# First projection of a two-layer decoder: input taken in halves of channels, with the loads, transposes and first weight reordered

## The chip, the cores and the metric

The kernel runs on one core of one Trainium2 chip. Its time is the device time of one execution in microseconds (us), given as the median of several executions; lower is better. Beside the timed runs there is one profiled execution, whose span goes from its first to its last instruction. Engines are named as in the profile: PE (TensorE, matmuls; PEld its weight loads), ACT (ScalarE), DVE (VectorE), POOL (GpSimd), SP (SyncE, which here only issues transfers).

## The reference

A decoder trunk of two layers works on x of 512 tokens by 1024 channels in float32. Layer 0 is dilated sliding-window attention and a gated feed-forward with a short convolution; layer 1 is a forgetting attention over keys and values made once, and the same feed-forward. Only the very beginning matters here: the norm of the input and the first projection.

```python
def rms_norm(x, g):
    x32 = x.astype(jnp.float32)
    y = x32 * lax.rsqrt(jnp.mean(x32 * x32, axis=-1, keepdims=True) + EPS)
    return (y * g.astype(jnp.float32)).astype(x.dtype)

def dilated_mixer(xn, w_qkv, w_o, cos, sin):
    B, T, _ = xn.shape
    qkv = xn @ w_qkv                      # (512, 1024) @ (1024, 2304)
    q, k, v = jnp.split(qkv, 3, axis=-1)
    q = apply_rope(q.reshape(B, T, A_HEADS, HEAD_DIM), cos, sin)
    ...
# reference(): mix = dilated_mixer(rms_norm(h, g[0]), w_qkv_a[l], w_o_a[l], cos, sin), h = x at first
```

## The kernel before, in words

**Precision.** Every float32 operand of a matmul is split in a high part, rounded to the matmul's format (`fp32r`), and a low part, the rest. A product is three matmuls: high by high, high by low, low by high (`mm3`, L282 to L285).

**The first stage** computes q and k of the first head group for all 512 tokens: 4 blocks of 128 tokens (b) by 512 columns, each the sum over 8 chunks of 128 channels (kc), so 4 x 8 x 3 = 96 matmuls into four PSUM banks (`qk_ps`). Channels must lie on the partitions, so x is transposed on PE in 128 x 128 pieces, 4 x 8 = 32 of them, four to a PSUM bank (`xt_ps`). ACT copies a bank to the high part (`xah`, line L1268), DVE subtracts that from the bank for the low part (`xal`, L1272). The gains are folded into the weight: ACT scales a piece of w by the gain of its channel (`W.high`, L64), DVE makes the low part in one instruction (`W.low`, L82). The rows' own factor (the root mean square, `rstd0`, L1060 to L1062: a square and sum on ACT, a root, a reciprocal on DVE) is applied when the bank is read (`qk_post`, L1094), where POOL then rotates q and k (rope, L1100 to L1103).

**Weights.** The class `Weights` goes through a list of pieces of 128 x 1024 numbers (512 KB). Pieces 0 to 3 are the first stage's weight, two chunks kc each, loaded as two transfers of 256 KB; pieces 4 and 5 are v of the same group; from 6 on come the other groups. `load(n)` issues transfers up to piece n, `high`, `low`, `split` make the parts, `get` hands a pair to PE. The first six raw pieces lie in tiles of their own (`wearly`, two pieces to a tile `early[i]`).

**What sets the order.** There is no scheduler: the program's order is each engine's order (`manual_schedule`), and an engine that waits holds all that stands behind it. All transfers of this stage are issued by SP in program order: the gains of the norm (4 KB, L235), x block 0 (512 KB, L225), pieces 0 and 1, x block 1, piece 2, x block 2, piece 3, the rope table, x block 3, and so on. There are eight semaphores for such transfers; a transfer is issued only when the one eight places ahead of it has landed.

**PE's order at the start.** Three warm-up matmuls on zeros (L243, 128 x 512 bf16), the transpose of the gains (L260), five more warm-ups, the eight transposes of block 0, two warm-ups, then qk of block 0, kc 0, 1 and 2; the eight transposes of block 1; block 0, kc 3; block 1, kc 0 to 3; transposes of block 2; block 0, kc 4 and 5, block 1 the same; transposes of block 3; kc 6 and 7 of blocks 0 and 1; then all 24 matmuls of block 2 and all 24 of block 3. After that comes the v projection (`v_proj0`, tile `v_ps`), with transposes of the rotated q and k in between (`qk_transpose`, L1109, blocks 0 and 1 after half of it, 2 and 3 at its end).

**POOL's order** after its masks: rope of block 0 and of block 1, eight copies that bring blocks 0 and 1 in the order of tokens of the other groups (`reorder`, L1083), rope of blocks 2 and 3, four more such copies.

Of the kernel before, what the change touches and what calls it, by code (L numbers as in the profile page):

```python
# [9 lines left out]
F32 = mybir.dt.float32  # L10
F32R = mybir.dt.float32r
BF16 = mybir.dt.bfloat16
AF = mybir.ActivationFunctionType
ALU = mybir.AluOpType

D = 1024
T = 512
NB = 4
KD = D // 128
# [98 lines left out]
def trunk_kernel(ctx, tc, x, norm_gains, w_qkv_a, w_o_a, w_q_b, w_o_b, kv_norm, w_kvf, b_f,  # L118
                 w_up, conv_w, conv_b, w_down, rope, out):
    nc = tc.nc  # L120
    act, dve, pool, pe, sp = nc.scalar, nc.vector, nc.gpsimd, nc.tensor, nc.sync
# [8 lines left out]
    def t8(shape, dt=F32, name="t8"):  # L130
        return p8.tile(shape, dt, tag="t8", name=name)

    def t4(shape, dt=F32, name="t4"):
        return p4.tile(shape, dt, tag="t4", name=name)
# [4 lines left out]
    def bank(shape, name="bank"):  # L139
        return psp.tile(shape, F32, tag="ps", name=name)  # L140
# [4 lines left out]
    xv, outv = x[0], out[0]  # L145
# [62 lines left out]
    early = []  # L208
# [8 lines left out]
    W = Weights(nc, new_raw, lambda: t8([128, 2, 1024], F32R, name="w"), pieces)  # L217
# [3 lines left out]

    h = cst.tile([128, NB, D], F32, name="h")

    def load_x(b):
        sp.dma_start(h[:, b, :], xv[b * 128:(b + 1) * 128, :])  # L225

    def load_gain(src, name):
        t = t4([128, D], name=name)
# [2 lines left out]

    eps_t = cst.tile([128, 1], F32, name="eps_t")
    dve.memset(eps_t, EPS)
    g_row = sml.tile([8, 128], F32, tag="grow", name="g_row", bufs=1)
    sp.dma_start(g_row, norm_gains[0, 0].rearrange("(k p) -> k p", p=128))  # L235

    zero = t2([128, 512], BF16, name="zero")
    dve.memset(zero, 0.0)
# [2 lines left out]
    def warm_up(n):  # L241
        for i in range(n):
            pe.matmul(warm, zero[:, 0:128], zero, start=True, stop=True)  # L243
    load_x(0)
    W.load(2)
    load_x(1)
    W.load(3)
    load_x(2)
    W.load(4)
    rp = t4([128, 8, 32], name="rope")  # L250
    sp.dma_start(rp, rope)
    load_x(3)
    act.activation(sml.tile([128, 1], F32, tag="sd", name="warm"), eps_t, AF.Sqrt)

    ident = cst.tile([128, 128], F32, name="ident")
    make_identity(nc, ident)

    warm_up(3)
    pg0 = bank([128, 8], name="g_ps")
    pe.transpose(pg0, g_row, ident[:8, :8])  # L260
    gcol0 = sml.tile([128, 8], F32, tag="gcol0", name="gcol0", bufs=1)
    dve.tensor_copy(gcol0, pg0)
    warm_up(5)

    def columns(*ks):
        return [gcol0[:, k:k + 1] for k in ks]
# [4 lines left out]
    for s in range(2):  # L271
# [6 lines left out]
    pool.affine_select(mask0[:, 128:256], mask0[:, 128:256], pattern=[[-1, 128]], compare_op=ALU.is_ge,  # L278
                       fill=NEG, base=0, channel_multiplier=1)
    same = cst.tile([128, 4], F32, name="same")  # L280

    def mm3(o, ah, al, bh, bl, first, last, shared=False):  # L282
        pe.matmul(o, ah, bh, start=first, stop=False, skip_group_check=shared)  # L283
        pe.matmul(o, ah, bl, start=False, stop=False, skip_group_check=shared)  # L284
        pe.matmul(o, al, bh, start=False, stop=last, skip_group_check=shared)  # L285
# [57 lines left out]
    def new_xT(name):  # L343
        hi = [t8([128, 4, T], F32R, name=f"{name}h{i}") for i in range(2)]
        lo = [t8([128, 4, T], F32R, name=f"{name}l{i}") for i in range(2)]
        return hi, lo
# [17 lines left out]
    def xs(xT, kc, s):  # L364
        return xT[0][kc // 4][:, kc % 4, s], xT[1][kc // 4][:, kc % 4, s]
# [686 lines left out]
    xT = new_xT("xa")  # L1052
# [4 lines left out]
    def rstd0(b):  # L1057
        ss, sd = small(1, "s1"), small(1, "sd")
        junk = t2([128, D], BF16, name="junk")
        act.activation(junk, h[:, b, :], AF.Square, scale=1.0 / 32, accum_out=ss)  # L1060
        act.activation(sd, ss, AF.Sqrt, bias=eps_t)
        dve.reciprocal(rt[:, 0, b:b + 1], sd)  # L1062

    def factors_out():
        act.dma_start(rd.rearrange("(b p) -> p b", p=128), rt[:, 0])
# [10 lines left out]
    def reorder(copy, *blocks, parts=(0, 1)):  # L1076

        for i in parts:
            for b in blocks:
                for part in range(2):  # L1080
                    src = by_fourth(xT[part][i][:, :, b * 128:b * 128 + 128])
                    dst = xP[part][i].rearrange("p k (r l) -> p k r l", r=4)[:, :, :, b * 32:b * 32 + 32]
                    copy(dst, src.bitcast(F32))  # L1083

    def ax(g, b, kc):
        return xs(xP if g else xT, kc, slice(b * 128, b * 128 + 128))
# [3 lines left out]
    def qk_post(g, b, o):  # L1090
        if b == 0:
            qks[g] = t8([128, 4, 8, HD], name=f"qk{g}")
        qk = qks[g][:, b]
        act.activation(qk.rearrange("p a d -> p (a d)"), o, AF.Identity, scale=factor(g, b))  # L1094
        tu = t2([128, 2, 8, 16], name="tu")
        rb = 4 * min(g, 1) + b
        c2 = rp[:, rb, None, 0:16].to_broadcast([128, 8, 16])
        s_lo = rp[:, rb, None, 16:24].to_broadcast([128, 8, 8])
        s_hi = rp[:, rb, None, 24:32].to_broadcast([128, 8, 8])
        pool.tensor_tensor(tu[:, 0], qk[:, :, 0:16], c2, ALU.mult)  # L1100
        pool.tensor_tensor(tu[:, 1, :, 0:8], qk[:, :, 8:16], s_lo, ALU.mult)
        pool.tensor_tensor(tu[:, 1, :, 8:16], qk[:, :, 0:8], s_hi, ALU.mult)
        pool.tensor_tensor(qk[:, :, 0:16], tu[:, 0], tu[:, 1], ALU.add)  # L1103
# [151 lines left out]
    W.ahead = 1  # L1255
    ws, qk_banks = {}, {}

    def transposed0(b):
        pts = []
        for i in range(2):  # L1260
            pt = bank([128, 4, 128], name="xt_ps")
            for k in range(4):
                pe.transpose(pt[:, k, :], h[:, b, (4 * i + k) * 128:(4 * i + k + 1) * 128], ident)
            pts.append(pt)
        return pts

    def high0(b, pts, i):
        act.copy(xT[0][i][:, :, b * 128:b * 128 + 128], pts[i])  # L1268

    def low0(b, pts, i):  # L1270
        s = slice(b * 128, b * 128 + 128)
        dve.tensor_tensor(xT[1][i][:, :, s], pts[i], xT[0][i][:, :, s].bitcast(F32), ALU.subtract)  # L1272

    def qk0(b, *kcs):
        if b not in qk_banks:
            qk_banks[b] = bank([128, T], name="qk_ps")
        for kc in kcs:
            s, k = kc // 2, kc % 2
            if s not in ws:
                ws[s] = [t.rearrange("p (k c) -> p k c", k=2) for t in W.get()]  # L1280
            wh, wl = ws[s]
            ah, al = ax(0, b, kc)
            mm3(qk_banks[b], ah, al, wh[:, k, :], wl[:, k, :], kc == 0, kc == KD - 1)

    def split0(b):
        pts = transposed0(b)
        for i in range(2):
            high0(b, pts, i)
            low0(b, pts, i)

    pts = transposed0(0)
    warm_up(2)
    high0(0, pts, 0)
    low0(0, pts, 0)
    W.high()
    W.low()
    high0(0, pts, 1)
    qk0(0, 0, 1)
    W.high()
    W.low()  # L1300
    low0(0, pts, 1)
    qk0(0, 2)
    pts = transposed0(1)
    for i in range(2):
        high0(1, pts, i)
        low0(1, pts, i)
    qk0(0, 3)
    rstd0(0)
    W.split(3)
    qk0(1, 0, 1, 2, 3)  # L1310
    split0(2)
    rstd0(1)
    qk0(0, 4, 5)
    W.split(4)
    qk0(1, 4, 5)
    split0(3)
    qk0(0, 6, 7)
    qk_post(0, 0, qk_banks[0])
    W.split(5)
# [8 lines left out]
    rstd0(2)  # L1328
    rstd0(3)
    reorder(pool.tensor_copy, 0, 1)  # L1330
    qk0(2, *range(8))
    qk_post(0, 2, qk_banks[2])
    factors_out()
    qk0(3, *range(8))
    W.ahead = 4
    qk_post(0, 3, qk_banks[3])
    reorder(pool.tensor_copy, 2, 3, parts=(1,))
# [377 lines left out]
    for n in range(N + 3):  # L1715
        live = n < N
        if live:
            j, i = units[n]
# [96 lines left out]
```

## Time and profile before

| | us |
|---|---|
| median of 3 runs | 1103.9 |
| lowest and highest of them | 1103.11, 1105.02 |
| the profiled execution's own time | 1105.67 |
| its span | 1103.9 |
| PE busy in it | 1094.8 |

A row of the order of time gives the start, how long the first to the last of the row's instructions took, engine, line, operation, the tiles it writes and reads, shapes and count, and in brackets how long the engine had been idle and what ended that. A row of the busy times by stretch gives the stretch, its length, the busy time of PE, PEld, DVE, ACT and POOL with the instructions begun, the clock, the share of the transfer engines and GB/s. A row of groups ends with count, busy time and mean ns of one, and idle time before. A row of the chain is a start, a length and what ran. Matmuls are pipelined: the distance from one start to the next is what one costs in a row of them, not its own duration.

### The profile page before, as it was taken

How to read it: one execution, taken by the hardware profiler on the slowest of the kernel's cores; microseconds unless marked ns; L12 is line 12 of the kernel's file. 1: busy time of each engine (PE TensorE's matmuls, PEld its weight loads, DVE VectorE, ACT ScalarE, POOL GpSimd, SP SyncE). 2: the span in 40 equal slices, each digit the busy share in tenths (PEclk: the TensorE clock that was granted, in tenths of full speed). 3: DMA queues.
4: the chain of work that ended last, by engine and by line, in shares of the span. 5: the costliest groups of instructions: out<-in, count | busy, mean ns of one | idle time of the engine just before them, and what ended most of it. 6: DMA issues, size and time to landing. Idle time of an engine off the chain costs nothing.

```text
span 1103.9 us, 18085 instructions
## 1 busy us (share of the span) xinstructions
PE 1094.8 (99%) x6605; PEld 952.2 (86%) x6605; DVE 873.4 (79%) x1497; ACT 671.0 (61%) x1115; POOL 172.6 (16%) x245
## 2 busy tenths in 40 slices
PE   9999999999999999999999999999999999999997
PEld 6988889899999988888878888889899999988886
DVE  5697788888788779898587666868888788779894
ACT  6654565656666647576552488746656666647572
POOL 2632000311111211000000211100311111211000
PEclk9999999999999999999999999999999999999999
DMA  9699864378887979884446866784368887989872
GB/s 322 175 351 411 321 185 135 79 184 197 205 189 181 248 249 321 319 294 145 134 153 211 274 185 193 241 261 133 82 178 200 201 192 181 235 269 319 315 248 77
DMA packets 191553, 242.66 MB, mean 220 GB/s; under 512 B 12784, under 2 KB 138728, under 8 KB 191464
## 3 DMA queue, kind: packets, MB, share of 16 engines
q1 hardware_dynamic: 175848, 189.33, 53.0%
q0 software_dynamic: 14944, 52.18, 20.7%
q8 instruction: 52, 0.85, 0.3%
q14 instruction: 37, 0.30, 0.1%
q10 hardware_dynamic: 672, 0.00, 0.0%
HBM read 172.37 MB, written 39.73 MB: 192 GB/s over the span
## 4 chain that ended last, share of the span: by engine, by line
PE 94%; DMA 2%; issue 2%; DVE 1%; ACT 1%; SPq 0%; POOL 0%; DVEq 0%; POOLq 0%; ACTq 0%
PE up L285 12%; PE up L283 12%; PE up L284 12%; PE acc L283 9%; PE acc L284 9%; PE acc L285 9%; PE v_ps L283 2%; PE v_ps L285 2%; PE v_ps L284 2%; PE qk_ps L284 2%; PE qk_ps L283 2%; PE qk_ps L285 2%; PE first L285 1%; PE first L283 1%; PE first L284 1%
## 5 line engine op out<-in xcount | busy, mean ns | idle before, releaser
L283 PE MATMUL acc<-w 128*128 128x512 f32 (+1 forms) x311 | 120.6, 388 | 0.3 <-DVE mix L332 0.3
L285 PE MATMUL acc<-w 128*128 128x512 f32 (+1 forms) x311 | 120.4, 387 | 0.0
L284 PE MATMUL acc<-w 128*128 128x512 f32 (+1 forms) x267 | 103.2, 387 | 0.0
L285 PE MATMUL up<-xsh,w 128*128 128x256 f32 x352 | 99.7, 283 | 0.2 <-DMA w<-wsum 0.2
L283 PE MATMUL up<-xsh,w 128*128 128x256 f32 x352 | 99.6, 283 | 0.0
L284 PE MATMUL up<-xsl,w 128*128 128x256 f32 x352 | 99.6, 283 | 0.0
L78 DVE TENSOR_TENSOR w<-wraw,w 128x1024 fp32r<-128x1024 f32 x62 | 82.2, 1349 | 21.2 <-ACT w L60 16.8
L620 ACT ACTIVATE bb<-up,conv 128x512 f32<-128x512 f32 x80 | 59.7, 776 | 59.3 <-DVE up L1007 48.4
L284 PE MATMUL up<-xbl,w 128*128 128x512 f32 (+1 forms) x276 | 93.5, 339 | 0.0
L284 PE MATMUL up<-xcl,w 128*128 128x512 f32 (+1 forms) x276 | 93.5, 339 | 0.0
L283 PE MATMUL up<-xbh,w 128*128 128x512 f32 (+1 forms) x276 | 93.5, 339 | 0.0
L283 PE MATMUL up<-xch,w 128*128 128x512 f32 (+1 forms) x276 | 93.5, 339 | 0.0
L285 PE MATMUL up<-xbh,w 128*128 128x512 f32 (+1 forms) x276 | 93.4, 339 | 0.0
L285 PE MATMUL up<-xch,w 128*128 128x512 f32 (+1 forms) x276 | 93.4, 338 | 0.0
L60 ACT CAST w<-wraw 128x1024 fp32r<-128x1024 f32 x81 | 83.3, 1048 | 16.5 <-PE v_ps L284 6.9
L283 PEld LDWEIGHTS acc<-w 128*128 128x128 f32 x311 | 58.4, 188 | 12.5 <-DVE mix L332 0.7
L285 PEld LDWEIGHTS acc<-w 128*128 128x128 f32 x311 | 58.4, 188 | 11.9
L285 PEld LDWEIGHTS up<-xsh,w 128*128 128x128 f32 x352 | 67.6, 192 | 0.4 <-DMA w<-wsum 0.4
L283 PEld LDWEIGHTS up<-xsh,w 128*128 128x128 f32 x352 | 67.6, 192 | 0.0
L284 PEld LDWEIGHTS up<-xsl,w 128*128 128x128 f32 x352 | 67.6, 192 | 0.0
L621 DVE SCALAR_TENSOR_TENSOR bb<-up,conv,bb 128x511 f32<-128x511 f32 x80 | 59.5, 743 | 6.5 <-ACT bb L620 6.5
L623 DVE SCALAR_TENSOR_TENSOR bb<-up,conv,bb 128x510 f32<-128x510 f32 x80 | 59.9, 748 | 2.8
(310 smaller groups left out, 3110.1 us busy)
## 6 DMA issues: line engine op xcount, KB each, us to landing
wraw<-in_w_up_dram SPq DMA_DIRECT2D x88, 512.0 KB
w<-wraw POOLq DMA_DIRECT2D x32, 512.0 KB, 6.4
dT<-dsums SPq DMA_DIRECT2D x28, 512.0 KB
w<-wsum POOLq DMA_DIRECT2D x24, 512.0 KB, 5.6
dsums<-in_w_down_dram SPq DMA_DIRECT2D x22, 512.0 KB
dsums<-in_w_down_dram SPq DMA_DIRECT2D x44, 256.0 KB
hD<-hc POOLq DMA_DIRECT2D x44, 256.0 KB, 7.0
dact<-hD SPq DMA_DIRECT2D x44, 256.0 KB
```

Source lines behind the costliest of these rows:

```text
L60: (copy or self.nc.scalar.copy)(pair[:, 0], raw)
L78: self.nc.vector.tensor_tensor(pair[:, 1], raw, pair[:, 0].bitcast(F32), ALU.subtract)
L283: pe.matmul(o, ah, bh, start=first, stop=False, skip_group_check=shared)
L284: pe.matmul(o, ah, bl, start=False, stop=False, skip_group_check=shared)
L285: pe.matmul(o, al, bh, start=False, stop=last, skip_group_check=shared)
L620: act.activation(bb[:, s, :], ps, AF.Identity, bias=cp[:, 3, ch:ch + 1], scale=cp[:, 2, ch:ch + 1])
L621: dve.scalar_tensor_tensor(bb[:, s, 1:], ps[:, :T - 1], cp[:, 1, ch:ch + 1], bb[:, s, 1:], ALU.mult, ALU.add)
L623: dve.scalar_tensor_tensor(bb[:, s, 2:], ps[:, :T - 2], cp[:, 0, ch:ch + 1], bb[:, s, 2:], ALU.mult, ALU.add)
```

## The change

Everything computed stays the same: 96 matmuls, 32 transposes, the same parts and scales. What changes is the size of x's transfers and the order.

- **Transfers.** x comes as eight halves (128 tokens by 512 channels, 256 KB). SP issues the first half of block 0 first, then piece 0, then the first halves of blocks 1, 2 and 3. The gains are issued by ACT. POOL copies one number from piece 0's first half into piece 1's place, so piece 1 is not issued before piece 0's first half has landed; it stands ahead of the second halves of blocks 0 and 1, piece 2, the second halves of blocks 2 and 3, the rope table and piece 3.
- **Warm-ups.** Four ahead of the gains' transpose and one behind the first transposes: five instead of ten.
- **Transposes** come by halves: four for block 0, four for block 1, eight for blocks 2 and 3; the second halves are taken for blocks 0 and 1 together, and for 2 and 3 together.
- **First weight.** Chunk 0 of piece 0 is scaled on DVE (`tensor_scalar`), chunk 1 on ACT as before; high and low parts come chunk by chunk between the parts of x.
- **PE's matmuls**: block 0 and 1 on kc 0 and 1 one by one as the parts come (`one0`), then kc 0 and 1 of blocks 2 and 3, kc 2 and 3 of blocks 0 and 1, the second halves' transposes of 0 and 1, kc 2 and 3 of blocks 2 and 3, the second halves' transposes of 2 and 3; kc 4 to 7 of blocks 0 and 1, then of block 2, then of block 3. The statistics of blocks 0 and 1 stand further back on ACT.

```diff
-    def load_x(b):
-        sp.dma_start(h[:, b, :], xv[b * 128:(b + 1) * 128, :])
+    def load_x(i, *blocks):
+        s = slice(i * 512, (i + 1) * 512)
+        for b in blocks:
+            sp.dma_start(h[:, b, s], xv[b * 128:(b + 1) * 128, s])
...
+    load_x(0, 0)
     g_row = sml.tile([8, 128], F32, tag="grow", name="g_row", bufs=1)
-    sp.dma_start(g_row, norm_gains[0, 0].rearrange("(k p) -> k p", p=128))
+    act.dma_start(g_row, norm_gains[0, 0].rearrange("(k p) -> k p", p=128))
...
-    load_x(0)
-    W.load(2)
-    load_x(1)
-    W.load(3)
-    load_x(2)
-    W.load(4)
+    W.load(1)
+    load_x(0, 1, 2, 3)
     rp = t4([128, 8, 32], name="rope")
-    sp.dma_start(rp, rope)
-    load_x(3)
...
-    warm_up(3)
+    warm_up(4)
     pg0 = bank([128, 8], name="g_ps")
     pe.transpose(pg0, g_row, ident[:8, :8])
...
-    warm_up(5)
...
+    pool.tensor_copy(early[0][:, 1, 0:1], early[0][:, 0, 0:1])
+    W.load(2)
+    load_x(1, 0, 1)
+    W.load(3)
+    load_x(1, 2, 3)
+    sp.dma_start(rp, rope)
+    W.load(4)
...
+    def split0(i, *blocks):
+        pts = [transposed0(b, i) for b in blocks]
+        for b, pt in zip(blocks, pts):
+            high0(b, i, pt)
+            low0(b, i, pt)
+
+    def first_weight(k):
+
+        s, g = slice(512 * k, 512 * k + 512), columns(k)[0]
+        if k == 0:
+            dve.tensor_scalar(w0[:, 0, s], raw0[:, s], g, None, ALU.mult)
+        else:
+            act.activation(w0[:, 0, s], raw0[:, s], AF.Identity, scale=g)
+
+    def first_low(k):
+        s, g = slice(512 * k, 512 * k + 512), columns(k)[0]
+        dve.scalar_tensor_tensor(w0[:, 1, s], raw0[:, s], g, w0[:, 0, s].bitcast(F32), ALU.mult, ALU.subtract)
...
+    raw0, w0 = W.raw.pop(0), W.new_pair()
+    W.ready[0] = (w0[:, 0], w0[:, 1])
+    W.n_split = 1
+    pt = transposed0(0, 0)
+    warm_up(1)
+    high0(0, 0, pt)
+    first_weight(0)
+    first_low(0)
+    first_weight(1)
+    one0(0, 0, 0)
+    one0(0, 0, 1)
+    low0(0, 0, pt)
+    one0(0, 1, 0)
+    first_low(1)
+    one0(0, 0, 2)
+    split0(0, 1)
+    one0(0, 1, 1)
+    one0(0, 1, 2)
+    qk0(1, 0)
+    split0(0, 2, 3)
     W.high()
     W.low()
...
+    qk0(1, 1)
+    for b in (2, 3, 0):
+        qk0(b, *((2, 3) if b == 0 else (0, 1)))
+    qk0(1, 2, 3)
+    split0(1, 0, 1)
+    W.split(3)
+    qk0(2, 2, 3)
     rstd0(0)
-    W.split(3)
-    qk0(1, 0, 1, 2, 3)
-    split0(2)
+    qk0(3, 2, 3)
+    split0(1, 2, 3)
+    W.split(4)
     rstd0(1)
     qk0(0, 4, 5)
-    W.split(4)
     qk0(1, 4, 5)
-    split0(3)
     qk0(0, 6, 7)
...
-    qk0(2, *range(8))
+    qk0(2, 4, 5, 6, 7)
     qk_post(0, 2, qk_banks[2])
     factors_out()
-    qk0(3, *range(8))
+    qk0(3, 4, 5, 6, 7)
```

`one0(b, kc, n)` is one of the three matmuls of `mm3` for block b and chunk kc (n = 0 high by high, 1 x high by weight low, 2 x low by weight high), and `qk0` calls it for whole chunks.

More of the change, by code (lines that the diff above doesn't have):

```diff
@@ L1256, in trunk_kernel @@
     ws, qk_banks = {}, {}
[L1258 to L1270, printed above, removed]
-        s = slice(b * 128, b * 128 + 128)
-        dve.tensor_tensor(xT[1][i][:, :, s], pts[i], xT[0][i][:, :, s].bitcast(F32), ALU.subtract)
@@ L1274, in qk0, with transposed0, high0, low0 @@
-    def qk0(b, *kcs):
+    def transposed0(b, i):
+        pt = bank([128, 4, 128], name="xt_ps")
+        for k in range(4):
+            pe.transpose(pt[:, k, :], h[:, b, (4 * i + k) * 128:(4 * i + k + 1) * 128], ident)
+        return pt
+    def high0(b, i, pt):
+        act.copy(xT[0][i][:, :, b * 128:b * 128 + 128], pt)
+    def low0(b, i, pt):
+        s = slice(b * 128, b * 128 + 128)
+        dve.tensor_tensor(xT[1][i][:, :, s], pt, xT[0][i][:, :, s].bitcast(F32), ALU.subtract)
+    def split0(i, *blocks):
[3 more added lines that the diff above has]
+            low0(b, i, pt)
@@ new lines, in first_weight, with weight0 @@
+    def first_weight(k):
[7 more added lines that the diff above has]
+        dve.scalar_tensor_tensor(w0[:, 1, s], raw0[:, s], g, w0[:, 0, s].bitcast(F32), ALU.mult, ALU.subtract)
+    def weight0(s):
+        if s not in ws:
+            ws[s] = [t.rearrange("p (k c) -> p k c", k=2) for t in W.get()]
+        return ws[s]
@@ L1275, in qk0, with one0 @@
+    def one0(b, kc, n):
         if b not in qk_banks:
             qk_banks[b] = bank([128, T], name="qk_ps")
+        w, a = weight0(kc // 2), ax(0, b, kc)
+        pe.matmul(qk_banks[b], a[n == 2], w[n == 1][:, kc % 2, :], start=kc + n == 0, stop=kc + n == KD + 1)
+    def qk0(b, *kcs):
         for kc in kcs:
[L1278 to L1294, printed above, removed]
+            for n in range(3):
+                one0(b, kc, n)
+    raw0, w0 = W.raw.pop(0), W.new_pair()
+    W.ready[0] = (w0[:, 0], w0[:, 1])
+    W.n_split = 1
+    pt = transposed0(0, 0)
@@ L1295, in trunk_kernel @@
+    warm_up(1)
[14 more added lines that the diff above has]
+    split0(0, 2, 3)
     W.high()
     W.low()
[L1297 to L1306, printed above, removed]
@@ L1307, in trunk_kernel @@
-    qk0(0, 3)
+    qk0(1, 1)
[5 more added lines that the diff above has]
+    qk0(2, 2, 3)
     rstd0(0)
-    W.split(3)
-    qk0(1, 0, 1, 2, 3)
-    split0(2)
+    qk0(3, 2, 3)
+    split0(1, 2, 3)
+    W.split(4)
     rstd0(1)
     qk0(0, 4, 5)
-    W.split(4)
     qk0(1, 4, 5)
-    split0(3)
     qk0(0, 6, 7)
```

## The prediction

> **What bounds the kernel now.** I read the page first (share of the engines, then the chain that ended last), then the first 35 us in order of time, the busy times by stretch with the bytes moved, and last POOL's own order.
>
> ```profile
> span 1103.9 us, 18085 instructions
> PE 1094.8 (99%) x6605; PEld 952.2 (86%) x6605; DVE 873.4 (79%) x1497; ACT 671.0 (61%) x1115; POOL 172.6 (16%) x245
> PE 94%; DMA 2%; issue 2%; DVE 1%; ACT 1%; SPq 0%; POOL 0%; DVEq 0%; POOLq 0%; ACTq 0%
> ```
>
> PE is busy 99% and carries 94% of the chain; 9.1 us of the span are left without it. So a change in the first stage is worth what it does to one moment: when PE passes from the last `qk_ps` matmul to `v_ps`. Behind it nearly everything waits for PE and shifts with it.
>
> ```profile
> 0.74 0.40 SPq L235 DMA_DIRECT2D g_row<-in_norm_gains_dram  x1
> 1.20 0.36 SPq L225 DMA_DIRECT2D h<-in_x_dram  x1
> 1.22 1.46 PE L243 MATMUL warm<-zero 128*128 128x512 bf16 x3 [1.22 <-DVE zero L238]
> ...
> 2.61 0.27 PE L260 MATMUL g_ps<-ident,g_row 8*128 8x8 f32 x1
> 2.81 2.31 PE L243 MATMUL warm<-zero 128*128 128x512 bf16 x5
> 4.81 1.62 PEld L1263 LDWEIGHTS xt_ps<-ident,h 128*128 128x128 f32 x8 [0.59 <-DMA h<-in_x_dram]
> 4.92 1.92 PE L1263 MATMUL xt_ps<-ident,h 128*128 128x128 f32 x8
> 6.02 0.59 ACT L1268 CAST xah<-xt_ps 128x512 fp32r<-128x512 f32 x1 [3.79 <-PE xt_ps L1263]
> 6.50 1.34 ACT L64 ACTIVATE w<-wearly,gcol 128x512 fp32r<-128x512 f32 x2
> 6.63 0.82 PE L243 MATMUL warm<-zero 128*128 128x512 bf16 x2
> 6.64 0.69 DVE L1272 TENSOR_TENSOR xal<-xt_ps,xah 128x512 fp32r<-128x512 f32 x1 [3.55 <-ACT xah L1268]
> 7.26 1.42 DVE L82 SCALAR_TENSOR_TENSOR w<-wearly,gcol,w 128x512 fp32r<-128x512 f32 x2
> 7.28 0.50 PE L283 MATMUL qk_ps<-w,xah 128*128 128x512 f32 x1
> ...
> 9.11 0.40 PE L285 MATMUL qk_ps<-w,xal 128*128 128x512 f32 x1
> 9.61 1.46 ACT L64 ACTIVATE w<-wearly,gcol 128x512 fp32r<-128x512 f32 x2 [1.30 <-DMA wearly<-in_w_qkv_a_dram]
> 10.38 0.50 PE L283 MATMUL qk_ps<-w,xah 128*128 128x512 f32 x1 [0.87 <-ACT w L64]
> 11.67 0.87 PEld L1263 LDWEIGHTS xt_ps<-ident,h 128*128 128x128 f32 x8 [0.20 <-DMA h<-in_x_dram]
> 11.74 1.04 PE L1263 MATMUL xt_ps<-ident,h 128*128 128x128 f32 x8
> 12.53 0.48 PE L283 MATMUL qk_ps<-w,xah 128*128 128x512 f32 x1
> ```
> ```profile
> 34.31 0.28 PE L283 MATMUL v_ps<-w,xah 128*128 128x256 f32 x1
> ```
>
> The reader is to see three things. x of block 0 is there at 4.81, the first useful matmul runs at 7.28, and PE stands between 9.11 and 10.38 until ACT can scale the second weight, whose transfer came at 9.6. From 12.53 PE never stops: 87 of the 96 matmuls and 16 of the 32 transposes are left and take 34.31 - 12.53 = 21.8 us. And PE is slow at first: the eight transposes from 4.92 to 6.63 take 0.21 each, those from 11.74 to 12.53 0.10; the five warm matmuls from 2.81 to 4.92 take 0.42 each; the two from 6.63 to 7.28 take 0.65 together, so the pitch halved at about 7.05. (The clock column reads full from the start; the pitch is what counts.)
>
> **The change part by part.** *Input by halves, gains on ACT's queue.* The first half of x's block 0 takes the gains' place at 0.74 instead of 1.20, and has 0.26 MB instead of 0.52.
>
> ```profile
> 2.00:3.00 1.00, 1.00 (x4) 0.31 (x3) 0.08 (x1) 0.22 (x2) 0.17 (x1) 1.00 0.84 152
> 3.00:4.00 1.00, 1.00 (x3) 0.30 (x2) 0.09 (x1) 0.00 (x0) 0.00 (x0) 1.00 0.88 346
> 4.00:5.00 1.00, 1.00 (x4) 0.34 (x3) 0.00 (x0) 0.00 (x0) 0.00 (x0) 1.00 0.98 337
> 5.00:6.00 1.00, 1.00 (x7) 1.00 (x6) 0.00 (x0) 0.00 (x0) 0.00 (x0) 1.00 0.93 299
> 6.00:7.00 1.00, 1.00 (x5) 0.72 (x5) 0.36 (x1) 0.98 (x2) 0.00 (x0) 1.00 1.01 290
> 7.00:8.00 1.00, 0.78 (x3) 0.19 (x1) 1.00 (x3) 1.00 (x3) 0.00 (x0) 1.00 1.00 349
> 8.00:9.00 1.00, 0.94 (x4) 0.76 (x5) 0.67 (x2) 0.31 (x1) 0.00 (x0) 1.00 1.00 373
> ```
>
> The last column is GB/s. Before, 4.81 - 1.20 = 3.61 from issue to use; 0.26 MB less at 346 GB/s is 0.76 less, so it lands at 0.74 + 3.61 - 0.76 = 3.6. The first weight's halves follow at 4.35 and 5.1, the other three first halves by about 6.0, 6.8 and 7.6: x1's ends 1.05 MB into the queue, which these rows reach at 5.7, less 0.46 for the earlier start, plus the 0.7 by which x0 (0.52 MB, reached at 4.1) was usable after its bytes. The gains still come around 2.1, before the four warm matmuls end at 2.9. SP stops at the second weight until POOL's one-element copy, which waits for the first weight half: about 4.6. Behind that wait stand all later loads, but 0.79 MB of x halves are then queued, to about 7, so the engines don't run dry; that cover ends if the half comes over 1.5 us late.
>
> *First chain.* Four transposes start at 3.65; before, ACT's cast began 6.02 - 4.92 = 1.10 after the first one, so 4.75, done 5.34. Beside it DVE scales the first weight half. Nearest row:
>
> ```profile
> L1647 DVE TENSOR_SCALAR prob<-prob,rl 128x512 f32<-128x512 f32 x16 | 7.1, 484 | 0.3
> ```
>
> 4.35 + 0.48 = 4.9, hidden by the cast; on ACT it would cost 0.72, so even a slow DVE (0.69, the DVE subtract) hides. Low part: 0.75, 5.6. Matmuls at the slow pitch (0.43): 5.38, 5.81, 6.24 (ACT's second scaling, 5.23 to 5.97), 6.67 (x's low part, 5.53 to 6.25), end 7.1. Four transposes at full pitch end 7.5, two matmuls 8.0; then PE waits for block 1's cast (last transpose ends 7.7, plus 0.59: 8.4), runs two, waits 0.2 for its low part (9.1), and ends that matmul at 9.35. These waits are new, 0.6 in all, and are in the sum.
>
> *From there.* Nine matmuls and eight transposes are done at 9.35, against nine and sixteen at 12.53. Chain rows:
>
> ```profile
> 16.33 0.87 PE xt_ps L1263 x8
> 17.21 0.23 PE qk_ps L283
> ```
>
> So 21.8 + 0.87 = 22.65 remain: **the stage ends at 32.0, 2.3 earlier** than 34.31. Cover: the second weight is wanted at 9.35 + 0.87 + 15 x 0.23 = 13.7; it ends 2.1 MB into the queue, by the rows at 8.9 - 0.46 + 0.7 = 9.1, and needs 1.34 + 0.75 on ACT and DVE: 11.2, 2.5 us of cover. The statistics (L1060) move later on ACT; `qk_post` is the next to use them, and no matmul of the stage waits for it. Behind POOL's copy stands its rope work, wanted only after 20 us.
>
> *Clock.* Before, it opened 4.4 us after PE's last hole, which ends at 2.61. The two ends: if holes don't count, 1.22 + 4.4 = 5.6, and the same sum with a full pitch from there gives 31.5; if the count begins again after each, 5.4 + 4.4 = 9.8 (after the wait for the first cast) or 9.1 + 4.4 = 13.5 (after the last), and it gives 32.6 or 34.3, since each us at the slow pitch costs about half a us of matmuls. I take 7.05, the moment of the row above. [...]
>
> **Which run is this?** The profiled execution took 1105.67, its span 1103.9 and 1.8 around it; the median of the runs is 1103.9, the lowest 1103.11. The sum against itself is 1105.67 - 2.3 = 1103.4. But it had a late transfer: the second weight's first half ends 1.31 MB into the queue, reached at 6.6, so usable at 7.3 by x0's 0.7, and it was used at 9.61. Without these 2 us ACT takes it up after its cast at 8.3, the high part is there at 9.0, the low part 9.7, the three matmuls end 10.2, the eight transposes 11.05 (x1, 2.1 MB into the queue, is there at 9.6): 1.5 ahead of 12.53, and the old stage ends at 32.8. The new order has 2.5 us of cover there and hardly feels it. So against a run with the late share the gain is 2.3, against one without it 32.8 - 32.0 = 0.8. I take the lowest run as one without: 1103.11 - 0.8 = **1102.3**, 1.6 below the median.
>
> **The rivals.** *Late share in every run* (for: the first bytes of a tensor may always be slow; against: the profiled time is above all three runs). Then the whole 2.3 stands against the median: 1101.6, with an early clock (31.5) 0.5 less, 1101.1.
>
> *The clock opens late*, because PE's start has holes (for: the stretch from 1.22 to 3.65 was about two thirds busy and didn't open it; against: from 3.65 the changed PE is idle 0.4 in 3.4). Opening at 9.8 to 13.5 ends the stage at 32.6 to 34.3: by the 32.8 of the lowest run 1102.9 to 1104.6, I take the middle, 1103.8. [...]
>
> *POOL becomes the wait: slower.*
>
> ```profile
> 23.04 0.46 POOL L1100 TENSOR_TENSOR tu<-qk,rope 128x128 f32<-128x128 f32 x1 [20.87 <-ACT qk L1094]
> ...
> 26.77 1.30 POOL L1083 CAST xph<-xah 128x512 fp32r<-128x512 f32 x1
> ...
> 34.82 1.14 POOL L1083 CAST xpl<-xal 128x512 fp32r<-128x512 f32 x1
> 35.92 0.47 POOL L1100 TENSOR_TENSOR tu<-qk,rope 128x128 f32<-128x128 f32 x1
> ...
> 41.13 0.46 POOL L1103 TENSOR_TENSOR qk<-tu 128x128 f32<-128x128 f32 x1
> ```
> ```profile
> 46.70 0.71 PE L1109 MATMUL qkT_ps<-ident,qk 128*128 128x128 f32 x5
> ```
>
> Block 0 is now complete 30 matmuls before the stage's end, not 54, so POOL's row (rope of two blocks, eight casts, rope of two) starts 11.3 - 5.5 = 5.8 before the end. At the old durations it takes 41.59 - 23.04 = 18.55 and ends 12.75 after the stage; PE wants block 3 at 46.70 - 34.31 + 0.44 = 12.83. So it decides from 18.6 us on. DVE's load beside it moves: if all casts take 1.30 the row is 0.8 longer, with all rope at the slow 2.9 a block 1.9. That last gives 1102.3 + 1.9 = 1104.2, above the median. For the other way: the last two ropes then meet an idler DVE, and block 1's 1.6 is the row.
>
> *The change doesn't do what it says*: SP's wait for POOL's copy fixes the order, so only in size; it lies inside the forecast.
>
> **How the numbers follow.** Forecast 0.46 (own range 1101.5 to 1103.1), late share in every run 0.27, late clock 0.18, POOL 0.09. The range reaches from an early clock with the late share (1101.1, less 0.3 for the steps' own spread) to a clock opening at 13.5 (1104.6): 1100.8 to 1104.6. A measurement can tell about 0.2% (2.2 us) from no change: faster means below 1101.7, which is most of the late-share case and a little of the forecast, 0.32; slower, above 1106.1, needs the clock past 15 us (stage end 35) and POOL's wait too, 0.06; within, 0.62.
>
> **What would show it.** In the changed profile: first transposes at 3.6, first `qk_ps` matmul near 5.4, no PE wait for `wearly` at all, waits of 0.4 and 0.2 for block 1's `xah` and `xal`, `v_ps` at 32.0, transposes of block 1 at 0.1 each (a clock open by 7). Wrong would be: transposes still at 0.21 after 9 us, SP's second weight issued after 6, or `qkT_ps` waiting for POOL. If `v_ps` starts at 32 and the median doesn't fall, the old runs had no late share.

## The result, and the profile after

| | us |
|---|---|
| before, median of 22 runs beside the changed kernel | 1103.88 (1103.11 to 1106.74) |
| after, median of 22 runs | 1106.93 (1104.99 to 1108.33) |
| after / before | 1.0022, 95% interval 1.0016 to 1.0028 |
| the profiled execution of after: own time, span | 1104.99, 1103.2 |

The kernel became 3.05 us slower; 1102.3 had been forecast, with 1104.6 as the upper end. The profiled execution of after is the lowest of its 22 runs and that of before (1105.67) lies above 21 of its 22, so the two traces side by side show a gain of 0.7. They show the mechanisms; their sizes need more runs.

Of the page of after, the span, the engines and the chain that ended last:

```profile
span 1103.2 us, 18083 instructions
PE 1093.7 (99%) x6600; PEld 952.3 (86%) x6600; DVE 878.0 (80%) x1498; ACT 670.5 (61%) x1114; POOL 173.5 (16%) x246
PE 97%; DMA 1%; DVE 1%; ACT 0%; issue 0%; DVEq 0%; ACTq 0%
```

PE still bounds the kernel. The first stage of after in order of time, PE only (columns as for before), and its first `v_ps` matmul:

```profile
3.60 1.12 PE L1266 MATMUL xt_ps<-ident,h 128*128 128x128 f32 x4 [0.29 <-DMA h<-in_x_dram]
5.39 1.66 PE L1303 MATMUL qk_ps<-w,xah 128*128 128x512 f32 x3 [0.25 <-ACT xah L1270]
7.28 1.05 PE L1266 MATMUL xt_ps<-ident,h 128*128 128x128 f32 x4
9.01 1.16 PE L1303 MATMUL qk_ps<-w,xah 128*128 128x512 f32 x2
10.01 0.40 PE L1303 MATMUL qk_ps<-w,xal 128*128 128x512 f32 x1
10.25 1.04 PE L1266 MATMUL xt_ps<-ident,h 128*128 128x128 f32 x8
...
32.77 0.28 PE L288 MATMUL v_ps<-w,xah 128*128 128x256 f32 x1
```

Transposes at 3.60 and the first `qk_ps` matmul at 5.39 are as forecast. But four transposes at 7.28 take 1.05 and eight at 10.25 take 1.04: the pitch halves only near 10 (the trace's record of the granted clock says 9.98; in before 7.06). `v_ps` starts 1.54 earlier than before, not 2.3. And what was gained is gone 17 us later:

```profile
45.14 1.32 PE L1114 MATMUL qkT_ps<-ident,qk 128*128 128x128 f32 x8
46.39 1.68 PE L1139 MATMUL s_ps<-qkT 64*128 64x128 f32 x16
49.55 0.50 PE L288 MATMUL qk_ps<-w,xph 128*128 128x512 f32 x1 [1.47 <-ACT V L1252]
```

The same three groups in before:

```profile
46.70 1.03 PE L1109 MATMUL qkT_ps<-ident,qk 128*128 128x128 f32 x8
47.66 1.68 PE L1134 MATMUL s_ps<-qkT 64*128 64x128 f32 x16
49.27 0.50 PE L283 MATMUL qk_ps<-w,xph 128*128 128x512 f32 x1
```

From the first `v_ps` matmul to the first one on `xph` before takes 14.96, after 16.78. Two things make up 1.76 of the 1.82 more: the last `qkT_ps` transposes take 1.32 instead of 1.03, and PE waits 1.47 until ACT has emptied the banks of `v_ps` into V. ACT tells why. After, then before, ACT in order of time:

```profile
34.95 0.69 ACT L1099 ACTIVATE qk<-qk_ps,rt 128x512 f32<-128x512 f32 x1 [1.59 <-DVE rt L1067]
35.03 0.40 ACTq L1070 DMA_DIRECT2D rd<-rt  x1
...
42.91 1.17 ACT L1088 CAST xpl<-xal 128x512 fp32r<-128x512 f32 x1
47.92 0.36 ACTq L1073 DMA_DIRECT2D rt<-rd  x1
48.65 1.57 ACT L1252 ACTIVATE V<-v_ps,rt 128x256 f32<-128x256 f32 x4 [4.58 <-PE s_ps L1139]
```
```profile
31.08 0.39 ACTq L1065 DMA_DIRECT2D rd<-rt  x1
...
40.51 0.33 ACTq L1068 DMA_DIRECT2D rt<-rd  x1
...
42.92 0.87 ACT L1247 ACTIVATE V<-v_ps,rt 128x256 f32<-128x256 f32 x2
```

These two transfers are the round trip of the row factors: `factors_out` writes the 512 factors from SBUF to a small DRAM tensor, one 4-byte number at a time, and `factors_in` reads them back in the order of tokens of the other groups. Both are issued by ACT, and the read holds ACT's queue until the write has landed. The trace's record of landings shows it: the write's last share lands 0.02 before the read goes out, at 40.49 before and at 47.90 after. Before, the write goes out at 31.08 and the read at 40.51, while ACT still has copies to do: nobody notices. The write takes the factors of all four blocks. The statistics of blocks 2 and 3 keep their place in the program, behind the `qk_post` of block 1; but in the new order block 1 is complete later, and that `qk_post` runs at 28.36 instead of 24.45. So after, the write goes out at 35.03, the read at 47.92. ACT has been idle since 44.1 and stands there till 48.65, with V behind the read. The releaser that this row names (`s_ps`) isn't the cause: the V rows need only `v_ps` and `rt`, and `s_ps` comes later in PE's order than the `v_ps` matmuls.

### The profile page after: what moved, and what is told of

Its sections match the earlier page's. It is cut to its first block, busy times and chain, and to the rows that moved or that the text cites. A ratio compares the mean times of both kernels' runs of the same rounds, so it can differ in the third digit from the quotient of the medians.

```text
span 1103.2 us, 18083 instructions
## 1 busy us (share of the span) xinstructions
PE 1093.7 (99%) x6600; PEld 952.3 (86%) x6600; DVE 878.0 (80%) x1498; ACT 670.5 (61%) x1114; POOL 173.5 (16%) x246
## 4 chain that ended last, share of the span: by engine, by line
PE 97%; DMA 1%; DVE 1%; ACT 0%; issue 0%; DVEq 0%; ACTq 0%
PE up L288 13%; PE up L289 13%; PE up L290 13%; PE acc L288 9%; PE acc L290 9%; PE acc L289 9%; PE v_ps L290 2%; PE v_ps L288 2%; PE v_ps L289 2%; PE pT_ps L1688 2%; PE o_ps L1703 2%; PE s_ps L1654 2%; PE qk_ps L1303 2%; PE first L290 1%; PE first L288 1%; PE first L289 1%
```

## The experiments

The first theory was that the loss has two sources: the round trip's read, which holds ACT (A), and the clock, which opens late when warm-ups are gone (B). The rivals were either one alone, and POOL (C): its last rope instruction of block 3 ends at 45.76 where PE wants the block at 45.58, 0.44 after the row at 45.14:

```profile
45.30 0.46 POOL L1108 TENSOR_TENSOR qk<-tu 128x128 f32<-128x128 f32 x1
```

All kernels compute the same; none leaves work out. The lowest and highest times stand in brackets, and the last three columns are from each one's single profile: "clock" is the moment of full speed in the trace's clock record, and the giving-back is the time from the first `v_ps` matmul to the first on `xph`.

| kernel | median | before beside it | ratio (95%) | clock | `v_ps` | `v_ps` to `xph` |
|---|---|---|---|---|---|---|
| before | 1103.88 | | | 7.06 | 34.31 | 14.96 |
| after | 1106.93 | 1103.88 | 1.0022 (1.0016 to 1.0028) | 9.98 | 32.77 | 16.78 |
| 1 read late | 1105.28 (1103.42 to 1106.35) | 1104.01 | 1.0008 (0.9999 to 1.0017) | 10.43 | 33.38 | 15.23 |
| 2 factors early | 1104.88 (1102.99 to 1107.17) | 1104.01 | 1.0007 (0.9998 to 1.0016) | 12.95 | 34.59 | 15.34 |
| 3 two more warm-ups | 1104.87 (1103.63 to 1107.21) | 1104.01 | 1.0006 (0.9997 to 1.0015) | 5.04 | 32.90 | 15.23 |
| 4 = 2 + 3 | 1104.04 (1102.82 to 1105.65) | 1104.01 | 0.9998 (0.9989 to 1.0006) | 4.89 | 31.79 | 15.34 |
| 5 after again, one run | 1104.61 | 1103.88 | | 10.26 | 33.21 | 15.98 |
| 6 before, write late | 1104.13 (1103.17 to 1105.33) | 1103.88 | 1.0003 (0.9994 to 1.0013) | 6.32 | 33.16 | 14.95 |
| 7 before, five warm-ups | 1104.55 (1103.46 to 1106.52) | 1103.88 | 1.0009 (1.0000 to 1.0018) | 11.58 | 34.34 | 14.96 |
| 8 = 4 + POOL's copies later | 1103.60 (1102.47 to 1104.88) | 1103.88 | 0.9998 (0.9990 to 1.0007) | 4.30 | 31.84 | 14.95 |
| 9 after again, timed | 1105.55 (1103.30 to 1107.31) | 1104.25 | 1.0014 (1.0005 to 1.0023) | 4.85 | 32.19 | 15.82 |
| 10 after, no warm-ups | 1106.74 (1104.25 to 1108.08) | 1104.25 | 1.0023 (1.0013 to 1.0032) | 10.12 | 32.96 | 15.33 |
| 11 = 1 + 3 + POOL's copies later | 1103.45 (1102.89 to 1103.96) | 1104.25 | 0.9994 (0.9986 to 1.0003) | 4.74 | 32.17 | 14.95 |
| 12 the same again | 1103.67 (1103.01 to 1104.42) | 1104.21 | 0.9997 (0.9988 to 1.0006) | 4.74 | 31.76 | 14.95 |

Numbers 1 to 4 shared a chip, so did 5 to 8 and 9 to 11. No run of the changed kernel was timed beside 1 to 4, and only the single one of number 5 beside 6 to 8. So their medians tell how far they are from the kernel before; how far from the changed kernel is told within one comparison only by 9 to 11.

**1. The read alone, later.**

```diff
     reorder(act.copy, 2, 3, parts=(0,))
-    factors_in()
...
+    factors_in()
     wide_proj(1, "qk_ps", qk_post, [
```

> The changed kernel, with the read of the row factors (rt from rd, on ACT's queue) moved from ahead of the v projection to behind it. Nothing else differs. Theory A, the round trip: the factors' write to DRAM is issued 4 us later than before (35.0 against 31.1), lands at 47.9, and the read behind it holds ACT from 44.1 to 47.9, so the v banks are emptied at 48.7 and PE's next projection starts 1.5 us late. Then ACT empties the v banks by 44 and 47, PE goes from the scores to the projection without the 1.5 us wait, and the median falls by 1.5 or more, to 1105.4 or below; if the landing is usually later than in the one profile, by up to 3, to about 1104. Theory B, the clock: the five missing warm-up matmuls open the clock late (9.98 against 7.06 in the profiles) and that is the loss: nothing changes here, 1106.9.

The wait for V is gone (the giving-back falls from 16.78 to 15.23), so ACT at the read was that wait. The ratio is 1.0008, against 1.0022 in the first comparison and 1.0014 in number 9; what the wait is worth in the median this run alone doesn't settle. The rest of the loss is elsewhere.

**2. The write earlier instead.** The statistics of blocks 0 and 1 stand ahead of the second halves' split, those of 2 and 3 where 0 and 1 were, and `factors_out` behind `qk_post(0, 1)`.

```diff
     qk0(1, 2, 3)
+    rstd0(0)
+    rstd0(1)
     split0(1, 0, 1)
     W.split(3)
     qk0(2, 2, 3)
-    rstd0(0)
+    rstd0(2)
...
-    rstd0(1)
+    rstd0(3)
...
     qk_post(0, 1, qk_banks[1])
+    factors_out()
     W.split(6)
-    rstd0(2)
-    rstd0(3)
...
     qk_post(0, 2, qk_banks[2])
-    factors_out()
```

> The changed kernel, with the statistics of all four blocks taken earlier on ACT (blocks 0 and 1 ahead of the casts of their second halves, 2 and 3 where those of 0 and 1 stood) and the factors' write issued right after the bank of block 1 is read. Theory A: the write goes out at about 28 and lands by about 40, the read finds it done, ACT isn't held, no 1.5 us wait of PE near 48: median 1105.4 or below, like the run with the late read, and perhaps 0.5 better since ACT reads the banks of blocks 2 and 3 about a us earlier. If the eight-places rule makes SP wait for this write instead, the loads of later weights come late and a wait of PE for w shows near 60 to 80. Theory B: 1106.9 as before.

The same from the other end: write at 29.41, read at 39.08, no wait for V. But this profile shows B at its worst. The busy time of PE in stretches of 3.41 us, here (with one PE row in order of time behind it) and in after (columns: stretch, length, PE, PEld, DVE, ACT, POOL, clock, share of the transfer engines, GB/s):

```profile
2.72:6.13 3.41, 3.00 (x9) 1.60 (x8) 1.97 (x4) 0.72 (x2) 0.19 (x1) 1.00 0.96 280
6.13:9.54 3.41, 2.72 (x9) 1.91 (x8) 0.78 (x2) 0.97 (x2) 0.00 (x0) 1.00 0.99 332
9.54:12.95 3.41, 3.41 (x14) 2.59 (x12) 0.69 (x1) 0.82 (x2) 0.00 (x0) 1.00 1.04 364
...
7.18 0.80 PE L1303 MATMUL qk_ps<-w,xah 128*128 128x512 f32 x1 [0.69 <-ACT w L1288]
```
```profile
3.16:6.57 3.41, 2.87 (x9) 1.79 (x10) 2.29 (x5) 1.31 (x2) 0.19 (x1) 1.00 0.99 323
6.57:9.98 3.41, 3.41 (x11) 2.34 (x10) 1.12 (x2) 0.59 (x1) 0.00 (x0) 1.00 0.97 320
```

The stretches are cut to end where the clock opened, and are 3.41 us long because of the clock record: in the fourteen profiles the full-speed time in it has just three lengths, 1088.852, 1092.265 and 1095.678, 3.413 apart. In every profile the stretch before the opening had PE busy 3.08 or more; the stretch ahead of that one, in the seven with an opening at 7.06 or later, never more than 3.00. What decides the opening the traces don't show; that it goes by how busy PE was in such a stretch, and that the stretches lie differently from run to run, is my estimate from these numbers. The opening varied from 4.85 to 10.26 in three profiles of the changed kernel. In the new order PE stands 0.29 ahead of the row at 3.60 and 0.25 ahead of that at 5.39; in after both holes fall into the stretch from 3.16 to 6.57 (2.87, that is 3.41 less both), and the clock opened at the end of the next. In number 2 there is a third hole: the 0.69 at 7.18, a wait for the first weight's second half, is all that the stretch from 6.13 lacks, and the clock opened a stretch later again, at 12.95.

**3. Two warm-ups put back.**

```diff
     pe.transpose(pg0, g_row, ident[:8, :8])
+    warm_up(1)
...
     pt = transposed0(0, 0)
-    warm_up(1)
+    warm_up(2)
```

> The changed kernel with two more warm-up matmuls, one behind the gains' transpose (in the hole 3.3 to 3.6) and one behind the first four transposes (in the hole 4.9 to 5.4); seven instead of five. Theory B: PE is then busy without a hole from 1.2 to 6.8, the clock opens at 7 rather than 10, the first stage ends 0.7 earlier by the step-by-step sum, and, if the late clock were the whole loss of 3 us, the median falls to about 1104. Theory A: at most 0.7 of it moves PE to the same wait near 48 earlier, where it waits longer: 1106.9, within 0.3.

The clock opens at 5.04. `v_ps` starts only at 32.90 all the same, since this run met something the forecast left out:

```profile
7.47 0.50 PE L1304 MATMUL qk_ps<-w,xah 128*128 128x512 f32 x1 [1.28 <-ACT w L1289]
```

ACT scales the second half of the first weight as soon as it is there; here the last of its transfer's 16 shares came at 6.6, in after at 5.4. Such a wait for this half (0.2 to 1.3) shows in six of the eleven profiles with the new order, and in a seventh (number 1) one of 0.4 for the first half. Something else doesn't show: PE doesn't wait for V, although the read still stands ahead of it. The write took 11.0 here, from 35.16 to 46.16, and `v_ps` to `xph` is 15.23 as in number 1.

**4. Both.** The edits of 2 and 3 together.

> Both edits: factors early and seven warm-ups. Theory A: the wait near 48 is gone, so what the clock gives in the first stage (0.7) now reaches the end: 0.5 to 0.7 below the run with the early factors alone, about 1104.5, and near the kernel before. Theory B alone: like the run with the warm-ups alone.

`v_ps` starts at 31.79, earlier than the forecast's 32.0, and the loss is gone. Added to the other, each correction is worth another 0.8 by the medians (1104.88 and 1104.87 to 1104.04), which speaks against A alone or B alone; the intervals overlap. But it isn't a gain: 1104.04 against 1104.01. The profiled run is the lowest of its eleven. In its PE waits up to the scores stands one that the kernel before hasn't (number 2 has it too):

```profile
PE qkT_ps L1115 <- POOL qk L1109: 0.2, 1, 0.2
```

**5. The changed kernel, a second profile.** No edit.

> The changed kernel, unchanged, profiled a second time. Its first profile has the lowest of all its times (1104.99, median 1106.93), so it can't show what an ordinary run loses. Theory (clock): in an ordinary run the clock opens later than 9.98, near 13 as in the run with the statistics early (12.95), and v_ps starts at 34 to 34.6; with the late read of the factors behind it the own time is 1106.3 to 1107. Rival (round trip alone): the clock opens at 10 again, v_ps starts within 0.4 of 32.8, and a run that takes 1106 or more waits 2.5 or more for V.

1104.61, clock at 10.26, `v_ps` at 33.21, a wait for V of 0.67. The clock is the rival's, but the run is again one below the median of after, so it can't say what an ordinary run loses. It shows both sources varying: the wait for V is less than half of the first profile's.

**6. The late write in the kernel before.**

```diff
     qk_post(0, 2, qk_banks[2])
-    factors_out()
...
     reorder(act.copy, 2, 3, parts=(0,))
+    factors_out()
     factors_in()
```

> The kernel before; only factors_out moves, from behind qk_post(0, 2) to directly ahead of the read (factors_in). Theory (round trip of the factors): write and read stand next to each other, the write goes out near 39 to 41 instead of 31.08, lands 9 to 13 us later (8.8 to 12.9 in five profiles), so the read is issued at 48 to 54 instead of 40.51 and V is emptied at 49 to 55 where 48.7 is still free (in the changed kernel 48.65, plus 1.54 for its earlier stage, cost 1.5): PE waits 1 to 5 for V, and the median is 1 to 5 above the kernel before. Rival (only the first stage counts, the reads are hidden): no difference beyond 0.5.

No difference, but the experiment missed its aim:

```profile
33.41 0.40 ACTq L1065 DMA_DIRECT2D rd<-rt  x1
33.95 3.78 ACT L64 ACTIVATE w<-wraw,gcol 128x512 fp32r<-128x512 f32 x6
...
40.75 1.15 ACT L1083 CAST xpl<-xal 128x512 fp32r<-128x512 f32 x1
43.85 0.34 ACTq L1068 DMA_DIRECT2D rt<-rd  x1
44.24 0.84 ACT L1247 ACTIVATE V<-v_ps,rt 128x256 f32<-128x256 f32 x2 [2.34 <-PE v_ps L284]
```

The write went out at 33.41 and not behind the ten instructions that stand ahead of it, the last of which begins at 40.75: the issue ran ahead of them; why it could isn't shown. It landed in time. The run says nothing against A, and shows that a transfer's place in ACT's program doesn't by itself say when it is issued.

**7. Five warm-ups in the kernel before.**

```diff
     dve.tensor_copy(gcol0, pg0)
-    warm_up(5)
+    warm_up(1)
...
     pts = transposed0(0)
-    warm_up(2)
+    warm_up(1)
```

> The kernel before with five warm-ups instead of ten: three ahead of the gains' transpose, one behind it, one behind the first transposes. Theory (clock): PE then stands idle from about 3.2 to 4.8, the slow pitch lasts beyond 7.05, to 9 or later, and v_ps starts 0.5 to 2 later than with ten; the median is 0.5 to 2 above the kernel before. Rival (the warm-ups are filling, the changed kernel lost by its round trip alone): slow pitch to about 7.1 and no difference beyond 0.4.

```profile
5.15 1.97 PE L1263 MATMUL xt_ps<-ident,h 128*128 128x128 f32 x8 [1.73 <-DMA h<-in_x_dram]
...
11.79 1.04 PE L1263 MATMUL xt_ps<-ident,h 128*128 128x128 f32 x8
```

B without the rest of the change: the clock opens at 11.58, the median rises by 0.67, with an interval that begins at 1.0000; the profiled run is the slowest of the eleven. By the medians the five warm-ups are worth 0.7 in the old order.

**8. POOL too.** As 4, with four of POOL's copies of blocks 0 and 1 behind the rope of blocks 2 and 3.

```diff
-    reorder(pool.tensor_copy, 0, 1)
+    reorder(pool.tensor_copy, 0, 1, parts=(0,))
...
-    reorder(pool.tensor_copy, 2, 3, parts=(1,))
+    reorder(pool.tensor_copy, 0, 1, 2, 3, parts=(1,))
```

> The changed kernel with all three: statistics and factors early, two warm-ups put back, and POOL's second four copies for blocks 0 and 1 moved behind the rope of blocks 2 and 3. The run with the first two took 1104.04 against 1104.01 for the kernel before, and its profile showed a wait of 0.2 for POOL and a slower pitch of the qkT transposes, 0.38 together. Theory (POOL takes the rest of it): no wait for POOL, 0.2 to 0.4 below that run, about 1103.7, 0.3 below the kernel before. Rival (the late shares of the transfers take the rest, POOL's wait is hidden): 1104.0 again, with the qkT wait gone and PE standing 0.5 to 1.5 for the first weight's second half in the profile.

The giving-back falls from 15.34 to 14.95, as before the change; the profile puts 0.39 on POOL. The median is 0.28 below the kernel before: the right size, but inside the interval.

**9. The changed kernel, timed again.** No edit.

> The changed kernel, unchanged, timed on the chip of the last runs and profiled a third time. Its two profiles took 1104.99 and 1104.61, its median was 1106.93 on another chip. Theory (round trip and clock both vary from run to run, and the two profiles were lucky ones): the median is 1106 to 1107 again, 2 to 3 above the kernel before, and a profile in the middle of the times shows a wait for V of 2 or more, or a clock that opens past 11. Rival (the loss belongs to the other chip): a median within 1 of the kernel before.

A loss again, but 1.30 and not 2 to 3: between the two expectations. Its profile is a lucky run (1103.58 of 1103.30 to 1107.31):

```profile
1.44:4.85 3.41, 3.29 (x10) 1.33 (x8) 0.72 (x3) 1.68 (x3) 0.85 (x4) 1.00 0.94 261
```
```profile
32.19 0.28 PE L288 MATMUL v_ps<-w,xah 128*128 128x256 f32 x1
...
44.56 1.32 PE L1114 MATMUL qkT_ps<-ident,qk 128*128 128x128 f32 x8
...
48.01 0.50 PE L288 MATMUL qk_ps<-w,xph 128*128 128x512 f32 x1 [0.52 <-ACT V L1252]
```

With PE busy 3.29 in the stretch from 1.44 to 4.85, the unchanged change opens the clock at 4.85, with the same five warm-ups that gave 9.98 and 10.26. Then the stage ends at 32.19, close to the forecast's 32.0, and only A and C are left, beside a wait of 0.67 for the first weight.

**10. No warm-ups.**

```diff
-    warm_up(4)
     pg0 = bank([128, 8], name="g_ps")
...
     pt = transposed0(0, 0)
-    warm_up(1)
```

> The changed kernel with none of its five warm-ups: the suspected loss of the clock doubled. PE does nothing but the gains' transpose before the first transposes at 3.6. Theory (clock): it opens at 12 or later instead of 9.98; a us of slow pitch costs about half a us, so v_ps starts at 33.8 to 35 where x and the weights are in time, and the median is 0.5 to 2 above the changed kernel. Rival (the five don't count for the clock, which opens by itself 6 to 7 after the first transposes): no difference beyond 0.4 from the changed kernel.

1.19 above number 9, in the expected range, and the lucky runs are nearly gone: one of nine is under 1106, of number 9 eight of eleven. The profile shows the clock at 10.12 and not beyond 12, and `v_ps` at 32.96, so its rows aren't what was expected; of that run's 1106.9, 3.1 more than in number 9's profile arose behind the first `xph` matmul, as at

```profile
104.17 0.66 PE L1160 MATMUL pT_ps<-ident,p 128*128 128x128 f32 x4 [1.15 <-ACT qk L1098]
```

The times lean to B, though the intervals of 9 and 10 overlap; the one profile speaks neither for nor against it.

**11. The read late, seven warm-ups, POOL's copies later.** The edits of 1, 3 and 8; the statistics stay where the change put them.

> As the run with all three, but the statistics stay where the change put them, and only the read of the factors moves back behind v. If the changed kernel's loss at V is ACT standing at that read and nothing else, then it makes no difference by which end the round trip is taken off ACT: 1103.3 to 1104.1, no PE wait for V, within 0.5 of the run with all three (1103.6), though the write goes out near 35 and lands past 44. Rival (late statistics cost something besides: ACT's wait of 1.6 for the reciprocals, late qk_post, late rope): 0.8 or more above it, with a PE wait for POOL or for qk_ps banks in the profile.

```profile
32.17 0.28 PE L289 MATMUL v_ps<-w,xah 128*128 128x256 f32 x1
...
44.54 1.03 PE L1115 MATMUL qkT_ps<-ident,qk 128*128 128x128 f32 x8
...
47.12 0.50 PE L289 MATMUL qk_ps<-w,xph 128*128 128x512 f32 x1
```

The stage ends as in number 9 (32.17 and 32.19), but `xph` comes at 47.12, not 48.01, and the median is 2.1 lower in the same comparison. All eleven times lie within 1.07 us, where the changed kernel's spread over 4.0: most of what varied from run to run is out. No further cost of the late statistics shows.

**12. The same again.** No edit.

> The kernel of the run with the late read, seven warm-ups and the later copies once more, on whatever chip it falls. It took 1103.45 against 1104.25 (0.9994, 0.9986 to 1.0003). If the 0.8 that the shorter first stage was said to be worth is there once the round trip, the clock and POOL no longer take it back, it is 0.4 to 1.2 below the kernel before again, with its times within some 1.5 of each other. Rival (0.8 was that chip's): within 0.3 of the kernel before or above it.

0.54 below the kernel before, after 0.80. Each interval reaches past 1, so neither run alone settles it; the direction and size are those that the forecast gave for the shorter stage, 0.8.

## Why the prediction was wrong

**The step that failed** is this sentence: "The statistics (L1060) move later on ACT; `qk_post` is the next to use them, and no matmul of the stage waits for it." It looks no further than the stage, and so does the premise that behind it nearly everything shifts with PE. Behind that `qk_post` stood the write of the factors, behind the write a read that holds ACT, behind the read V, and behind V a projection on PE. A new wait with these four links cost 1.47, 0.67 and 0.52 in three profiles of after, priced at nothing; in numbers 3 and 10, which keep the links, it cost nothing, so it varies from run to run. The write goes out 3.95 later (35.03 against 31.08) and takes 3.46 longer (12.89 against 9.43), so a delay of 4 became one of 7.4; and for a given landing, the sooner the stage ends, the longer PE waits. Numbers 1, 2 and 11 show it by taking it away from both ends. The forecast missed by 4.6, and this step doesn't account for all of that: three further terms take their shares.

**The clock** was a rival and not the forecast, at a chance of 0.18 and a price of 32.6 to 34.3 for `v_ps`. The price holds roughly (32.77 at 9.98; 34.59 at 12.95 is 0.3 above its end). What the rival called two thirds busy is, in the trace of before, 2.43 of the 3.41 from 0.24 to 3.65, and its 3.4 reach from 3.65 to 7.06, where full speed begins there. The chance was wrong in kind: 7.05 was carried over from one trace as if it were a property of the kernel, but the three profiles of the changed kernel opened at 9.98, 10.26 and 4.85, and neither 4.4 from PE's start at 1.22 nor 4.4 from a hole gives that 4.85; four of five profiles of the order with five warm-ups (after, numbers 1, 2, 5 and 9) drew 9.98 or later. Only in after did the order's own holes do that alone. In numbers 1, 2 and 5 a late share of the first weight emptied a stretch further, by 0.41, 0.69 and 0.39; without it these stretches (3.61 to 7.02, 6.13 to 9.54, 3.44 to 6.85), busy 2.87, 2.72 and 2.77, would have been busy 3.16 to 3.41 (an estimate by adding), and in number 8 the clock opened after one busy 3.08. By that estimate the late clock is in good part the late share again. Seven warm-ups drew 4.3 to 5.0 five times out of five, after stretches that ended before any such wait.

**POOL** was priced to within 0.1 of deciding (12.75 against 12.83) and given 0.09. It decided, by 0.3: `qkT_ps` in 1.32 instead of 1.03, with a row of 18.8 (26.94 to 45.76) against the 18.55 of the sum. The mechanism was right; the margin was too small to be given so little.

**The late share** was put down to the second weight alone, where the new order has cover. In six of eleven profiles it hit the first weight's second half, which has none: 0.2 to 1.3. Since the first halves' own arrival was as computed (3.60, 5.39), only the spread of the transfers was left out.

**The baseline** held as far as one profile goes: the kernel before with its first stage untouched (number 6) shows `v_ps` at 33.16 (forecast 32.8 without a late share) in a run of 1104.08. **The rest of the sum** held where the clock opened early: a wait of 0.2 for block 1's high part (forecast 0.4) and none for its low part (forecast 0.2), `v_ps` at 31.76 to 32.19 in five of six such profiles, and 0.28, 0.80 and 0.54 below the kernel before in numbers 8, 11 and 12, where A, B and C are taken out, each inside its interval.

What adds up: the five profiles of the new order with five warm-ups end the stage at 32.77, 33.38, 34.59, 33.21 and 32.19, 33.2 in the mean, no earlier than number 6 with the old order (33.16). To that comes what is given back, 15.82 to 16.78 less 14.95, so 0.9 to 1.8 of loss; 1.30 was measured in number 9, 3.05 in the first comparison. That A, B and C together are the loss is shown by number 11 beside number 9, whose intervals don't overlap. **Open** is what made it 3.05 the first time: no run of the changed kernel near 1107 was profiled, and its three profiled runs lay at the low end of its times. A longer wait for V or an opening at 13 would do it; neither was seen in the changed kernel itself. A third candidate lies behind all this: from the first `xph` matmul to the end of the span the fourteen profiles take 1053.7 to 1056.8, although the program is the same there. The three of after take the least, 1053.7 to 1053.8, before takes 1054.6 and number 7 1055.4; one wait of PE for ACT in layer 1's attention, near 695 us, is 0.7 in number 7, 0.3 in before and absent in the three of after. So an ordinary run of after may lose part of its 3.05 there; no run shows it. Open too is how the 2.1 us between 9 and 11 divide among A, B and C; the two profiles hold only 0.9 of them.

## What to carry to other kernels

When a step moves later, follow what it feeds to the end, past the stage that you are looking at: through every transfer that is issued behind it, and through everything that stands in that engine's queue behind a wait for the transfer. A warm-up that looks like filling can be what keeps the clock's opening the same from run to run (here within 0.8 us with seven, over 8 with five); judge it over many runs, not by one trace. Where a forecast rests on one trace, ask of each of its moments whether it belongs to the kernel or to that run.

## What the runs showed of the hardware

- The clock opened after a stretch with PE busy 3.08 (number 8) or more of 3.41; behind stretches busy 3.00 (numbers 2 and 7) it was still closed. In number 12 the stretch ahead of the opening held the gains' transpose (0.27) and four float32 transposes of x (1.06), and PE was busy throughout.

```profile
1.33:4.74 3.41, 3.41 (x11) 1.72 (x11) 0.62 (x2) 1.49 (x3) 0.96 (x4) 1.00 0.82 263
```

- The write of 2 KB in 4-byte pieces took 8.7 to 12.9 us until the read behind it could be issued (the eleven profiles with the read ahead of V), and on the whole longer the later it went out: 8.7 and 8.9 when issued at 26.6, 9.4 to 10.0 at 29 to 31, 10.4 at 33.4, 11.0 to 12.9 at 34.4 to 35.5.
- ACT issued a transfer 7.3 us ahead of the start of the last of ten instructions written before it (33.41 and 40.75, number 6).
